# GLA/retention decoder layer on Trainium2: down projections of two MLP groups as seven products, with the weights' sums made in memory by GpSimd's transfers

## The chip, the cores and the metric

The kernel runs on one core of one Trainium2 chip, in one launch. The metric is the device time of the launch in microseconds (us), on that core. A difference is judged by the median of several runs.

## The reference

One inference step of a decoder layer, D = 1024, for 512 prompt tokens and 8 x 8 sample tokens (576 tokens in all), in fp32:

```python
def layer(x, pos, s_gla, s_ret, mem_k, mem_v, ...):
    m, s_gla_new, s_ret_new = mixer_block(rmsnorm(x, g_pre_mix), ...)   # GLA and retention branches, 4 heads each
    x = x + rmsnorm(m, g_post_mix)
    x = x + rmsnorm(cross_attn(rmsnorm(x, g_pre_xa), mem_k, mem_v, w_xq, w_xo), g_post_xa)
    hf = rmsnorm(x, g_pre_ffn)
    x = x + rmsnorm(jnp.square(jax.nn.relu(hf @ w_up)) @ w_down, g_post_ffn)
    return x, s_gla_new, s_ret_new
```

The change concerns the last line but one: `w_up` is 1024 x 4096, `w_down` 4096 x 1024. Beside the tokens' output the layer returns the new states and the keys and values of the memory.

## The kernel before, in words

Activations lie transposed: features over the 128 partitions, 8 blocks (k) of them, and 576 tokens in two halves of 288 (NH). Every fp32 product is three fp32r matmuls: a factor is split into hi (a cast on ScalarE, L94) and lo (the rest, a subtraction on VectorE, L95), and hi x hi, lo x hi, hi x lo add up in PSUM (`mm3`, L251 to L253).

Weights come in tiles of 128 x 1024 (512 KB). `plan` lists them in the order of use; `wfetch` (L180) has SP load the next into a ring of 6 tiles (`wraw`), `wsplit` makes its hi and lo (`wh`, `wl`, a ring of 3), `wnext` hands out the next split tile, and `gemm_m` does 48 matmuls with it, on both halves of the tokens.

The stages in order: keys and values of the memory; eight mixer units (one head of GLA or of retention each, `UNITS`, in `mixers`); the mixer's output, cross attention; and the MLP in four groups of 1024 hidden features. In a mixer unit GpSimd does small work between the other engines' steps: the causal mask on the scores (an affine select, L978), the reciprocal roots `rs` (a power, L887), `ks` (L1076), the lo part of q (L99), a product on the gate G (L1140) and the sum into `merged` (L1149). A unit forms keys `kf`, values `vt`, then the first pair of gate products (L1133) and the second.

MLP group 0 is done plainly. For groups 1 to 3 the up products (h = relu(x w)^2) use seven products in place of eight (`sevenfold`, L281), Winograd's form of Strassen's scheme: the weights' features and the tokens' features are taken as 2 x 2 blocks, the tokens in two halves. With sums S1 to S4 of the activation's blocks (`fsh`, `fsl`, made once by `sums_f`) and sums of the weight's blocks, seven products of 12 matmuls each give the four result blocks, 84 matmuls for each of the four b of a group. The weight sums are made on VectorE there: `begin` takes two raw tiles and does four subtractions of 128 x 512 (`minus`, L213); two of the splits go to an extra tile `wq`. The down projections of groups 1 and 2 are plain, 8 k of 48 matmuls, each added into the accumulator `y3` by VectorE (L655); group 3's down products and the last norm end the kernel.

What sets the order is the program and a scheduler behind it, which takes each engine's instructions in program order in the main, but lets independent ones pass each other.

Of the kernel before, what the change touches and what calls it, by code (L numbers as in the profile page):

```python
# [13 lines left out]
P = 128  # L14
KT = 8
# [11 lines left out]


RING, STAY, RAW, SEVEN = 0, 1, 2, 3
# [29 lines left out]
def decoder_step(ctx, tc, xT, memT, ktc, vc, s_gla, s_ret, w_in, w_ga, w_a2, w_mix, w_xq, w_xk, w_xv, w_xo,  # L59
                 w_up, w_ups, w_down, vecs, cst, gam, y_out, mk_out, mv_out, sg_p, sr_p, sg_s, sr_s):  # L60
# [110 lines left out]
    wq = []  # L171
    units = []

    def wfetch():
        if plan and sum(m == SEVEN for _, m in raws) < 2:
            src, mode = plan.pop(0), RING
            if isinstance(src, tuple):
                src, mode = src
            raw = wp.tile([P, 1024], F32, name="wraw", bufs=N_RAW)
            nc.sync.dma_start(out=raw if len(src.shape) == 2 else raw.rearrange("p (k n) -> p k n", n=src.shape[2]), in_=src)  # L180
            raws.append((raw, mode))

    def wsplit():
        if units:
            units.pop(0)()
        elif raws:
            if raws[0][1] == SEVEN:
                begin()
                return
# [4 lines left out]
            pool = staying[-1] if mode == STAY else wp  # L194
            wh = pool.tile([P, 1024], F32R, name="wh")
            wl = pool.tile([P, 1024], F32R, name="wl")
            split(wh, wl, raw)
            ready.append((wh, wl))

    def halves(w):  # L200
        return w.rearrange("p (q n) -> p q n", q=2)

    def begin():


        while len(raws) < 2:
            wfetch()
        p0, p1 = (raws.pop(0)[0] for _ in range(2))
        t = wp.tile([P, 1024], F32, name="wraw", bufs=N_RAW)
        q0, q1, qt = halves(p0), halves(p1), halves(t)  # L210

        def minus(out, a, b):
            nc.vector.tensor_tensor(out=out, in0=a, in1=b, op=ALU.subtract)  # L213

        def ring(raw):
            wh = wp.tile([P, 1024], F32R, name="wh")
            wl = wp.tile([P, 1024], F32R, name="wl")
            split(wh, wl, raw)
            ready.append((wh, wl))

        def own(raw, o, n):
            w = wq[0][:, o:o + n], wq[0][:, o + n:o + 2 * n]
            split(*w, raw)
            ready.append(w)

        def unit_a():
            ring(p0)
            wfetch()

        units.extend([unit_a, lambda: ring(t), lambda: own(p1, 0, 1024),  # L230
                      lambda: minus(q1[:, 0], q1[:, 0], qt[:, 0]), lambda: own(q1[:, 0], 2048, 512)])
# [3 lines left out]
        wfetch()  # L235

    def wnext(n=P):

        while sum(len(r) == 2 for r in ready) < 2 and (raws or plan):
            while not units and plan and len(raws) + sum(len(r) == 1 for r in ready) < N_RAW - 1:  # L240
                n0 = len(raws)
                wfetch()
                if len(raws) == n0:
                    break
            if not raws and not units:
                break
# [26 lines left out]
    def sevenfold(x, p1, p5, u2, c11, c22, c12, c21):  # L273
# [375 lines left out]
    xnp = ctx.enter_context(tc.tile_pool(name="xnp", bufs=2))  # L649
# [4 lines left out]
    def add(out, a, b, op=ALU.add):  # L654
        nc.vector.tensor_tensor(out=out, in0=a, in1=b, op=op)  # L655

    def sums_f():

        for j in range(4):
# [5 lines left out]
            add(c2[:, 1], c2[:, 0], c2[:, 1])  # L665
            add(c2[:, 0], c1[:, 0], c2[:, 0], ALU.subtract)
            add(c1[:, 0], c2[:, 1], c1[:, 0], ALU.subtract)
            add(c1[:, 1], c1[:, 1], c1[:, 0], ALU.subtract)
            yield
            split(fsh[:, 2:4, j], fsl[:, 2:4, j], c2)  # L670
            split(fsh[:, 0:2, j], fsl[:, 0:2, j], c1)
            yield

    FQ = {"A11": (fh, fl, 0), "A12": (fh, fl, 1), "A22": (fh, fl, 3),
# [760 lines left out]
```

## Time and profile before

| what | us |
|---|---|
| median of 3 runs | 1197.8 (1197.7 to 1197.8) |
| the profiled execution | 1200.96 |
| its span, first to last instruction | 1199.2 |
| TensorE (PE) busy | 1168.2 |
| VectorE (DVE) busy | 747.2 |
| ScalarE (ACT) busy | 564.1 |
| GpSimd (POOL) busy | 152.7 |

The span is what the trace shows; the profiled execution's time holds it and what lies around it. Busy time is the sum over an engine's instructions with overlaps counted once; PE stands for matmuls, PEld for the loads of the stationary operand, SP for the engine that issues DMAs. L253 is line 253 of the kernel before; a tile's name stands in rows without its number.

### The profile page before, as it was taken

The numbers are of one execution on the slowest core, as the hardware profiler recorded it, in microseconds if no ns is written. First come the engines' busy times: TensorE is split into PE (matmuls) and PEld (weight loads), VectorE is DVE, ScalarE is ACT, GpSimd is POOL, SyncE is SP. The second block draws the span as 40 slices with busy tenths as digits, with TensorE's granted clock in tenths as the row PEclk, the third lists the DMA queues.
The fourth block names the chain that finished last, engine by engine and source line by source line (L and its number), as shares of the span: only waits on it lengthen the run. The fifth ranks groups of instructions, "written<-read, shape, count | busy, mean of one in ns | idle before, by whom it ended". The sixth has DMA issues, their size and how long they took to land.

```text
span 1199.2 us, 22007 instructions
## 1 busy us (share of the span) xinstructions
PE 1168.2 (97%) x9022; PEld 1134.6 (95%) x9022; DVE 747.2 (62%) x1334; ACT 564.1 (47%) x993; POOL 152.7 (13%) x165
## 2 busy tenths in 40 slices
PE   8999999999999999999999989999999999999995
PEld 7899999999999999999999878889999999999995
DVE  6756657566746574757777545686937546456565
ACT  5534546443444344524564534556527416515652
POOL 0521213122312231221001000000000000000000
PEclk9999999999999999999999999999999999999998
DMA  8762424232424232422745677653223223321631
GB/s 291 244 213 89 128 80 137 75 125 88 128 71 143 74 128 89 128 89 76 231 130 159 226 233 238 222 164 123 88 71 105 89 71 103 109 71 56 217 108 60
DMA packets 65621, 157.98 MB, mean 132 GB/s; under 512 B 5648, under 2 KB 34576, under 8 KB 65392
## 3 DMA queue, kind: packets, MB, share of 16 engines
q1 hardware_dynamic: 65520, 156.57, 41.0%
q8 instruction: 71, 1.16, 0.4%
q14 instruction: 30, 0.25, 0.1%
HBM read 140.29 MB, written 16.25 MB: 131 GB/s over the span
## 4 chain that ended last, share of the span: by engine, by line
PE 89%; DVE 4%; DMA 2%; ACT 2%; issue 1%; POOL 1%; SPq 0%; POOLq 0%; DVEq 0%; ACTq 0%
PE psg L251 22%; PE psg L252 22%; PE psg L253 22%; PE psa L281 6%; PE psg L281 3%; PE psa L251 2%; PE pso L281 2%; PE psa L252 1%; PE psa L253 1%; DMA wraw<-in_w_xo 1%; PE pso L1254 1%; DVE wl L95 1%; PE psa L1097 1%; PE pso L1092 1%; DVE res L527 1%
## 5 line engine op out<-in xcount | busy, mean ns | idle before, releaser
L251 PE MATMUL psg<-xh,wh 128*128 128x288 f32 x1280 | 381.5, 298 | 0.4 <-DVE t L819 0.3
L252 PE MATMUL psg<-xh,wl 128*128 128x288 f32 x1280 | 377.9, 295 | 0.8 <-DVE wl L95 0.8
L253 PE MATMUL psg<-xl,wh 128*128 128x288 f32 x1280 | 377.8, 295 | 0.0
L95 DVE TENSOR_TENSOR wl<-wraw,wh 128x1024 fp32r<-128x1024 f32 x196 | 241.8, 1234 | 93.0 <-ACT wh L94 92.3
L94 ACT CAST wh<-wraw 128x1024 fp32r<-128x1024 f32 x196 | 206.0, 1051 | 187.5 <-PE psg L253 105.7
L251 PEld LDWEIGHTS psg<-xh,wh 128*128 128x128 f32 x1280 | 240.8, 188 | 3.5 <-issue 2.2
L252 PEld LDWEIGHTS psg<-xh,wl 128*128 128x128 f32 x1280 | 240.9, 188 | 1.1 <-DVE wl L95 1.0
L253 PEld LDWEIGHTS psg<-xl,wh 128*128 128x128 f32 x1280 | 240.6, 188 | 0.1
L251 PE MATMUL psg<-hh,wh 128*128 128x288 f32 x512 | 152.2, 298 | 0.7 <-DVE y L761 0.6
L252 PE MATMUL psg<-hh,wl 128*128 128x288 f32 x512 | 150.6, 295 | 0.3 <-DVE wl L95 0.3
L253 PE MATMUL psg<-hl,wh 128*128 128x288 f32 x512 | 150.7, 295 | 0.0
L251 PEld LDWEIGHTS psg<-hh,wh 128*128 128x128 f32 x512 | 96.1, 188 | 1.6 <-issue 1.1
L252 PEld LDWEIGHTS psg<-hh,wl 128*128 128x128 f32 x512 | 96.0, 188 | 0.6 <-DVE wl L95 0.6
L253 PEld LDWEIGHTS psg<-hl,wh 128*128 128x128 f32 x512 | 96.1, 188 | 0.0
L333 POOL TENSOR_TENSOR rs<-ms,mhalf 96x3 f32<-96x3 f32 (+1 forms) x11 | 11.0, 999 | 525.1 <-DVE ms L326 525.1
L955 ACT COPY vt<-psg 128x512 f32<-128x512 f32 x16 | 9.4, 587 | 77.5 <-PE psg L253 77.5
L887 POOL TENSOR_TENSOR rs<-mv,mhalf 128x1 f32<-128x1 f32 x48 | 29.8, 621 | 112.7 <-DVE mv L882 64.6
L957 DVE COPY vd<-psg 128x128 f32<-128x128 f32 x32 | 7.8, 286 | 55.6 <-ACT vt L955 55.6
L251 PE MATMUL psg<-bh,wh 128*128 128x288 f32 x128 | 38.4, 300 | 1.6 <-ACT wh L94 1.1
L252 PE MATMUL psg<-fh,wl 128*128 128x288 f32 x128 | 38.9, 304 | 1.0 <-DVE wl L95 1.0
L655 DVE TENSOR_TENSOR y<-psg,y 128x576 f32<-128x576 f32 x16 | 12.1, 757 | 44.4 <-PE psg L253 44.4
L251 PE MATMUL psg<-fh,wh 128*128 128x288 f32 x128 | 39.0, 305 | 0.2 <-ACT fh L94 0.2
(331 smaller groups left out, 2413.0 us busy)
## 6 DMA issues: line engine op xcount, KB each, us to landing
wraw<-in_w_in SPq DMA_DIRECT2D x64, 512.0 KB, 3.7
wraw<-in_w_down SPq DMA_DIRECT2D x38, 512.0 KB, 4.3
wraw<-in_w_ups SPq DMA_DIRECT2D x24, 512.0 KB, 3.7
wraw<-in_ktc SPq DMA_DIRECT2D x16, 512.0 KB, 5.0
wraw<-in_vc SPq DMA_DIRECT2D x16, 512.0 KB, 4.5
wraw<-in_w_xq SPq DMA_DIRECT2D x14, 512.0 KB, 4.3
wraw<-in_w_xo SPq DMA_DIRECT2D x14, 512.0 KB, 6.4
wraw<-in_w_up SPq DMA_DIRECT2D x14, 512.0 KB, 4.5
```

Source lines behind the costliest of these rows:

```text
L94: nc.scalar.copy(hi, src)
L95: nc.vector.tensor_tensor(out=lo, in0=src, in1=f32(hi), op=ALU.subtract)
L251: nc.tensor.matmul(out, ah, bh, start=first, stop=False)
L252: nc.tensor.matmul(out, al, bh, start=False, stop=False)
L253: nc.tensor.matmul(out, ah, bl, start=False, stop=last)
L281: nc.tensor.matmul(out, s[:, q, k], m[:, k], start=first and k == i == 0, stop=k == 3 and i == 2, skip_group_check=True)
L527: nc.vector.tensor_tensor(out=res[:, kk, c], in0=y[:, kk], in1=rj, op=ALU.add)
L655: nc.vector.tensor_tensor(out=out, in0=a, in1=b, op=op)
L887: nc.gpsimd.tensor_tensor(out=rs[:t], in0=mv[:t], in1=mhalf[:t, 0:1], op=ALU.pow)
L1092: nc.tensor.matmul(so[32 * j:32 * j + 8, o], qsd[:, b * 8:b * 8 + 8], s0[:, j], start=False, stop=True, skip_group_check=True, tile_positi ...
L1097: nc.tensor.matmul(U[:, j * 256:(j + 1) * 256], kst[g][:, 2 * bp + j, :], vst[g], start=True, stop=True)
L1254: nc.tensor.matmul(acc[rows, :256], x(h), w[:, h], start=first, stop=last, skip_group_check=True, tile_position=(0, 32 * h))
```

## The change

The sums of the weights are no longer made by VectorE at their use. The host lays out the weights of five groups of products (up 1, down 1, up 2, down 2, up 3) as blocks b11, b12, b21, b22 of 20 b (`w_sev`). During the mixers GpSimd issues DMAs from memory to memory that form, for ten pairs of b, three sums per b in internal tensors `t_sev`: t1 = b11 + b12, t2 = (t1 + b22, b12 + b22), t4 = t2[0] + b21. A pair takes eight transfers of 512 KB (64 x 2048 elements): four copies and four that add to what lies there. `sums` is called four times in each mixer unit and issues the steps that `SUMS_AT` and `SUM_STEPS` give for that call. A pair begins with a copy of one fresh element of the tile just made (`pace`) and its transfer of 1 x 1 into each of two sums' places, which the next copies overwrite.

With the sums in memory, `sevenfold` reads its weights as tiles of two 128 x 512 blocks (60 half-tile loads from `w_sev`, 80 from `t_sev`; a fourth tile of each b holds t4 alone, mode LAST), and it is now also used for the down projections of groups 1 and 2. Their activation is h: A11 and A12 go to `ha`, A22 to a free part of `fh`, the sums S1 to S4 to `hh` and `hl` (`pairs`). The seven products come in another order, and in a down group's first b A12 comes straight after A11 (`late`). `begin`, `units` and `wq` are gone. In all there are 8607 matmul instructions instead of 8703; GpSimd's queue goes from 170 instructions to 280, SP's from 347 to 447.

```diff
-RING, STAY, RAW, SEVEN = 0, 1, 2, 3
+RING, STAY, RAW, LAST = 0, 1, 2, 3
+N_SEV = 20
+SUMS_AT = (2, 5, 7, 10, 12, 15, 17, 20, 22, 25)
+SUM_STEPS = (0, 0, 1, 1, 2, 3, 4, 5)
...
-    def seven(w, b0):
-        return [(w[b0 + b][:, kh], SEVEN) for b in range(4) for kh in range(2)]
+    def seven(b0):
+        out = []
+        for n in range(b0, b0 + 4):
+            g, i = n // 2, n % 2
+            b = [w_sev[q, n] for q in range(4)]
+            t1, t2, t4 = t_sev[g]
+            out += [((b[0], t1[i]), RING), ((t2[0, i], t2[1, i]), RING), ((b[2], b[3]), RING), ((t4[i],), LAST)]
+        return out
     plan += whole(w_up) + rest(whole(w_up), 0) + whole(w_down)
     for g in range(1, 4):
-        plan += seven(w_ups, 4 * (g - 1))
-        plan += whole(w_down, 4 * g) + (rest(whole(w_down, 12), 0) if g == 3 else [])
+        plan += seven(8 * (g - 1))
+        plan += seven(8 * g - 4) if g < 3 else whole(w_down, 4) + rest(whole(w_down, 4), 0)
+    steps = {}
+    for g, at in enumerate(SUMS_AT):
+        b11, b12, b21, b22 = (w_sev[q, 2 * g:2 * g + 2] for q in range(4))
+        t1, t2, t4 = t_sev[g]
+        for n, (dst, src, plus) in zip(SUM_STEPS, (
+                (t1, b11, 0), (t2[1], b12, 0), (t1, b12, 1), (t2[1], b22, 1),
+                (t2[0], t1, 0), (t2[0], b22, 1), (t4, t2[0], 0), (t4, b21, 1))):
+            steps.setdefault(at + n, []).append((dst, src, plus))
+    clock = [0]
+    pace = perm.tile([1, 1], F32, name="pace")
+    def sums(after):
+        if clock[0] in SUMS_AT:
+            t1, t2, _ = t_sev[SUMS_AT.index(clock[0])]
+            nc.gpsimd.tensor_copy(pace, after[0:1])
+            for t in (t1[0], t2[1, 0]):
+                nc.gpsimd.dma_start(out=t[0:1, 0:1], in_=pace)
+        for dst, src, plus in steps.pop(clock[0], ()):
+            nc.gpsimd.dma_start(out=dst, in_=src, max_dma_last_dim=8192, **({"accum_op": ALU.add} if plus else {}))
+        clock[0] += 1
...
+            if isinstance(src, tuple):
+                for i, t in enumerate(src):
+                    nc.sync.dma_start(out=raw[:, i * 512:(i + 1) * 512], in_=t)
...
+            n = 512 if mode == LAST else 1024
+            pool = wdp[0] if mode == LAST else staying[-1] if mode == STAY else wp
+            wh = pool.tile([P, n], F32R, name="wh")
+            wl = pool.tile([P, n], F32R, name="wl")
+            split(wh, wl, raw[:, :n])
...
-        minus(qt[:, 1], q1[:, 1], q0[:, 1])
-        minus(q0[:, 1], q0[:, 1], q0[:, 0])
-        minus(qt[:, 0], q1[:, 1], q0[:, 1])
...
+        def c11():
+            prod(b, wb, 0, "A12", True)
+            add(c1[:, 0], b, c1[:, 0])
         prod(acc, wa, 0, "A11", True)
-        p1(acc)
-        while units:
-            wsplit()
+        nc.scalar.copy(c1[:, 0], acc)
+        if late:
+            c11()
+        prod(c, wa, 1, "S1", True)
+        nc.scalar.copy(c2[:, 1], c)
+        wmore()
         wd = ready.pop(0)
-        prod(c, wa, 1, "S1", True)
-        p5(c)
-        if raws and raws[0][1] == SEVEN:
-            begin()
         prod(acc, wc, 0, "S2", False)
-        wsplit()
-        u2(acc)
-        prod(b, wb, 0, "A12", True)
-        more()
-        c11(b)
+        nc.scalar.copy(c1[:, 1], acc)
+        wmore()
+        prod(c, wb, 1, "S4", False)
+        add(c1[:, 1], c, c1[:, 1], ALU.subtract)
         prod(acc, wc, 1, "S3", False)
-        c22(acc)
-        prod(c, wb, 1, "S4", False)
-        c12(c)
-        more()
+        add(c2[:, 1], c2[:, 1], acc, ALU.subtract)
+        done22()
+        wmore()
+        if not late:
+            c11()
+        done1()
+        wmore()
         prod(acc, wd, 0, "A22", False)
-        more()
-        c21(acc)
+        done21(acc)
...
+    def pairs(c1, c2, sh, sl):
+        add(c2[:, 1], c2[:, 0], c2[:, 1], ALU.subtract)
+        add(c2[:, 0], c1[:, 0], c2[:, 0], ALU.subtract)
+        split(sh[:, 2:4], sl[:, 2:4], c2)
+        add(c1[:, 0], c2[:, 1], c1[:, 0], ALU.subtract)
+        add(c1[:, 1], c1[:, 1], c1[:, 0])
+        split(sh[:, 0:2], sl[:, 0:2], c1)
...
+        plain = g in (0, 3)
+        ha = None if plain else biga.tile([P, 2, 2, 4, NH], F32R, name="ha", tag="biga")
+        def xh7(n):
+            if n in SQ:
+                return hh[:, SQ[n]], hl[:, SQ[n]]
+            return (fh[:, 2], fl[:, 2]) if n == "A22" else (ha[:, 0, n == "A12"], ha[:, 1, n == "A12"])
...
+            def done22():
+                relu2(c2[:, 1])
+                if not plain:
+                    split(fh[:, 2, b], fl[:, 2, b], c2[:, 1])
+            def done1():
+                relu2(c1)
+                split(*((hh[:, 0:2, b], hl[:, 0:2, b]) if plain else (ha[:, 0, :, b], ha[:, 1, :, b])), c1)
+            def done21(ps):
+                relu2(c2[:, 0], ps)
+                if plain:
+                    split(hh[:, 2:4, b], hl[:, 2:4, b], c2)
+                else:
+                    pairs(c1, c2, hh[:, :, b], hl[:, :, b])
+            sevenfold(xf7, c1, c2, done1, done22, done21)
+        if plain:
+            break
+        for b in range(4):
+            c1, c2 = (hp.tile([P, 2, NH], F32, name="hr") for _ in range(2))
+            y = [y3[:, 2 * b:2 * b + 2, hc(half)] for half in range(2)]
+            def done21(ps):
+                nc.scalar.copy(c2[:, 0], ps)
+                add(y[1], y[1], c2)
+            sevenfold(xh7, c1, c2, lambda: add(y[0], y[0], c1), lambda: None, done21, b == 0)
...
+            sums(kf[:, 511:512])
...
+            sums(vt[:, 1, 511:512])
...
+            sums(G[:, 1, NT - 1:])
```

The places in the engines' queues where the transfers and the new products came to stand. First GpSimd, in the mixer unit from about 208 us of the trace on, before (ql is the lo part of q, sm the scores, klo and ks parts of the key):

```order
L99 TENSOR_TENSOR ql_2563<-qf_2561,qh_2562 128x512 [waits Activation_49]
L978 AFFINE_SELECT sm_2785<-sm_2785 128x128 [waits Activation_49]
L1076 TENSOR_TENSOR ks_2816<-klo_2811,cm_834 128x512 [waits DVE_49]
L978 AFFINE_SELECT sm_2850<-sm_2850 128x128 [waits Activation_49,Pool_49]
L1076 TENSOR_TENSOR ks_2880<-klo_2875,cm_834 128x512 [waits DVE_49,PE_49]
```

The same stretch with the change:

```order
L102 TENSOR_TENSOR ql_2588<-qf_2586,qh_2587 128x512 [waits Activation_49]
L201 DMA t_sev20<-in_w_sev 64x2048 [waits DMASW6_49]
L201 DMA t_sev21<-in_w_sev 64x2048 [waits DMASW7_49]
L201 DMA t_sev21<-t_sev20 64x2048 [waits DMASW0_49]
L201 DMA t_sev21<-in_w_sev 64x2048 [waits DMASW3_49,DMASW2_49]
L201 DMA t_sev22<-t_sev21 64x2048 [waits DMASW3_49]
L1003 AFFINE_SELECT sm_2815<-sm_2815 128x128 [waits Activation_49]
L1101 TENSOR_TENSOR ks_2846<-klo_2841,cm_835 128x512 [waits DVE_49]
L201 DMA t_sev22<-in_w_sev 64x2048 [waits DMASW4_49]
L1003 AFFINE_SELECT sm_2880<-sm_2880 128x128 [waits Activation_49]
L1101 TENSOR_TENSOR ks_2910<-klo_2905,cm_835 128x512 [waits DVE_49,PE_49]
```

Five transfers have come between ql and the first mask, and a sixth between the first `ks` and the second mask; each of them waits in the queue for earlier ones (DMASW). The next rows of GpSimd's queue, from the unit's masks on to its first roots, before:

```order
L978 AFFINE_SELECT sm_2942<-sm_2942 128x128 [waits Activation_49,Pool_49]
L887 TENSOR_TENSOR rs1_2933<-mv_2930,mhalf_85 128x1 [waits DVE_49]
L978 AFFINE_SELECT sm_3034<-sm_3034 128x128 [waits Activation_49]
L887 TENSOR_TENSOR rs1_3025<-mv_3022,mhalf_85 128x1 [waits DVE_49]
L887 TENSOR_TENSOR rs1_3116<-mv_3113,mhalf_85 128x1 [waits DVE_49,Pool_49]
L887 TENSOR_TENSOR rs1_3141<-mv_3138,mhalf_85 128x1 [waits DVE_49,Pool_49]
```

With the change:

```order
L1003 AFFINE_SELECT sm_2972<-sm_2972 128x128 [waits Activation_49,Pool_49]
L910 TENSOR_TENSOR rs1_2963<-mv_2960,mhalf_85 128x1 [waits DVE_49]
L197 COPY pace_112<-G_2778 1x1 [waits DVE_49]
L199 DMA t_sev30<-pace_112 1x1 [waits Pool_49]
L1003 AFFINE_SELECT sm_3064<-sm_3064 128x128 [waits Activation_49]
L199 DMA t_sev31<-pace_112 1x1
L910 TENSOR_TENSOR rs1_3055<-mv_3052,mhalf_85 128x1 [waits DVE_49]
L201 DMA t_sev30<-in_w_sev 64x2048 [waits DMASW6_49]
L201 DMA t_sev31<-in_w_sev 64x2048 [waits DMASW7_49,DMASW1_49]
L910 TENSOR_TENSOR rs1_3153<-mv_3150,mhalf_85 128x1 [waits DVE_49]
L910 TENSOR_TENSOR rs1_3178<-mv_3175,mhalf_85 128x1 [waits DVE_49,Pool_49]
```

The next pair's first element, its two transfers and the pair's first two copies now stand between the masks and the roots (`rs`).

The third place is TensorE at the border from group 1's up products to its down projection, before (`psg` is the accumulator of a plain product):

```order
L251 MATMUL psg_11291<-hh_10785,wh_11214 128x288
L252 MATMUL psg_11291<-hh_10785,wl_11215 128x288
L253 MATMUL psg_11291<-hl_10786,wh_11214 128x288
L251 MATMUL psg_11291<-hh_10785,wh_11214 128x288 [waits Activation_49]
L252 MATMUL psg_11291<-hh_10785,wl_11215 128x288
L251 MATMUL psg_11347<-hh_10785,wh_11287 128x288 [waits DVE_49]
L252 MATMUL psg_11347<-hh_10785,wl_11288 128x288
L253 MATMUL psg_11347<-hl_10786,wh_11287 128x288
```

With the change, from the last A22 matmul on (`psa_11480` takes A11, `pso_11481` A12; `ha` and `hh` hold h):

```order
L280 MATMUL psa_11340<-fl_9469,wh_11371 128x288
L280 MATMUL psa_11480<-ha_10903,wh_11391 128x288
L280 MATMUL psa_11480<-ha_10903,wl_11392 128x288
L280 MATMUL psa_11480<-ha_10903,wh_11391 128x288 x2
L280 MATMUL psa_11480<-ha_10903,wl_11392 128x288
L280 MATMUL psa_11480<-ha_10903,wh_11391 128x288 x2
L280 MATMUL psa_11480<-ha_10903,wl_11392 128x288
L280 MATMUL psa_11480<-ha_10903,wh_11391 128x288
L280 MATMUL pso_11481<-ha_10903,wh_11452 128x288 [waits DVE_49,Activation_49]
L280 MATMUL pso_11481<-ha_10903,wl_11453 128x288 [waits DVE_49]
L280 MATMUL pso_11481<-ha_10903,wh_11452 128x288 x2
L280 MATMUL pso_11481<-ha_10903,wl_11453 128x288
```

and six rows on:

```order
L280 MATMUL pso_11481<-ha_10903,wh_11452 128x288 x2
L280 MATMUL pso_11481<-ha_10903,wl_11453 128x288
L280 MATMUL pso_11481<-ha_10903,wh_11452 128x288
L280 MATMUL psa_11480<-ha_10903,wh_11391 128x288 [waits Activation_49]
L280 MATMUL psa_11480<-ha_10903,wl_11392 128x288
L280 MATMUL pso_11481<-ha_10903,wh_11452 128x288
```

Before, the matmul that waits for the fourth block (k of block b = 3) is passed by the next k's; now A11's first three blocks and A12's come first, and A11's fourth behind them.

## Rows read from the trace of the kernel before

**Rows 1.** The page: its span and the engines' busy time.

```profile
span 1199.2 us, 22007 instructions
...
PE 1168.2 (97%) x9022; PEld 1134.6 (95%) x9022; DVE 747.2 (62%) x1334; ACT 564.1 (47%) x993; POOL 152.7 (13%) x165
```

Columns of the next group: stretch, its length, busy us of PE, PEld, DVE, ACT, POOL (instructions), granted clock, DMA share, GB/s.

**Rows 2.** Busy time by stretch, the MLP: a down stage, the up stage behind it.

```profile
938.00:990.00 52.00, 52.00 (x393) 51.86 (x392) 24.30 (x30) 12.33 (x16) 0.00 (x0) 1.00 0.20 62
990.00:1035.00 45.00, 45.00 (x337) 44.75 (x337) 30.23 (x40) 29.55 (x51) 0.00 (x0) 1.00 0.39 118
```

A row of a timeline has the start, the duration, engine, line, operation, out<-in, sizes and count; in brackets the idle time before it and what ended that.

**Rows 3.** TensorE's timeline at the borders of the stages.

```profile
893.03 0.29 PE L281 MATMUL psa<-fh,wh 128*128 128x288 f32 x1
...
938.28 0.29 PE L281 MATMUL psa<-fl,wq 128*128 128x288 f32 x1
938.41 0.30 PE L251 MATMUL psg<-hh,wh 128*128 128x288 f32 x1
...
989.57 0.29 PE L281 MATMUL psa<-fh,wh 128*128 128x288 f32 x1
...
1034.64 0.30 PE L251 MATMUL psg<-hh,wh 128*128 128x288 f32 x1
...
1085.80 0.29 PE L281 MATMUL psa<-fh,wh 128*128 128x288 f32 x1
```

**Rows 4.** The timeline of ScalarE and VectorE behind the up stage of group 1.

```profile
940.15 1.24 ACT L94 CAST hh<-hr 128x576 fp32r<-128x576 f32 x2
...
940.84 1.43 DVE L95 TENSOR_TENSOR hl<-hr,hh 128x576 fp32r<-128x576 f32 x2 [2.76 <-ACT hh L94]
```

A row of the waits: what waited, for what; us in all, times, the longest.

**Rows 5.** TensorE's waits, 70 to 560 us, then 893 to 1086 us.

```profile
PE psa L969 <- ACT T L1008: 0.8, 1, 0.8
PE psg L251 <- DVE t L819: 0.3, 1, 0.3
...
PE psa L281 <- ACT hr L727: 0.2, 1, 0.2
```

**Rows 6.** VectorE's subtractions on raw weights: ns of one (least, median, most).

```profile
L213 DVE TENSOR_TENSOR wraw<-wraw x48: 680/692/695, 859.5 to 1120.5; 128x512 f32<-128x512 f32 x48
```

**Rows 7.** SP's queue: its longest wait.

```profile
SPq L180 <- DVE wl L95: 658.0, 139, 12.3
```

**Rows 8.** GpSimd's timeline in the mixer unit from 208 us on.

```profile
208.07 1.29 POOL L99 TENSOR_TENSOR ql<-qf,qh 128x512 fp32r<-128x512 f32 x1 [5.28 <-ACT qh L98]
226.17 0.29 POOL L978 TENSOR_SCALAR_AFFINE_SELECT sm<-sm 128x128 f32<-128x128 f32 x1 [16.82 <-ACT sm L977]
...
254.48 0.55 POOL L887 TENSOR_TENSOR rs<-mv,mhalf 128x1 f32<-128x1 f32 x1 [2.42 <-DVE mv L884]
255.75 0.55 POOL L887 TENSOR_TENSOR rs<-mv,mhalf 128x1 f32<-128x1 f32 x1 [0.72 <-DVE mv L885]
```

**Rows 9.** TensorE and VectorE in the same unit: who uses mask and root.

```profile
233.89 0.28 PE L251 MATMUL psa<-vh,sh 128*128 128x256 f32 x1
...
257.80 0.38 PE L1029 MATMUL psa<-idn,on 128*128 128x128 f32 x2
...
256.34 0.48 DVE L893 TENSOR_SCALAR on<-pso,rs 128x256 f32<-128x256 f32 x1 [0.73 <-POOL rs L887]
```

**Rows 10.** The timeline where the first and last fresh element are made.

```profile
115.46 0.82 DVE L1133 SCALAR_TENSOR_TENSOR G<-psg,vec,t 128x576 f32<-128x576 f32 x1 [2.07 <-ACT t L1132]
...
470.82 0.59 ACT L955 COPY vt<-psg 128x512 f32<-128x512 f32 x1 [4.83 <-PE psg L253]
```

**Rows 11.** DMA issues: count, KB each, median us from issue to landing.

```profile
wraw<-in_w_in SPq DMA_DIRECT2D x64, 512.0 KB, 3.7
...
wraw<-in_w_xk SPq DMA_DIRECT2D x8, 512.0 KB, 7.4
...
res<-out_y SPq DMA_DIRECT2D x8, 288.0 KB, 5.5
...
vec<-in_vecs SPq DMA_DIRECT2D x1, 38.0 KB, 1.8
```

**Rows 12.** Busy time by stretch, in the mixers.

```profile
200.00:250.00 50.00, 50.00 (x394) 48.86 (x393) 30.16 (x72) 25.70 (x53) 9.16 (x13) 1.00 0.32 100
```

**Rows 13.** VectorE's copies, 100 to 520 us: busy us, mean ns, idle time before.

```profile
L922 DVE COPY qf<-t 128x512 f32<-128x512 f32 x3 | 1.3, 427 | 4.0 <-POOL t L903 4.0
```

More of the change, by code (lines that the diff above doesn't have):

```diff
@@ L170, in decoder_step @@
     raws, ready, staying = [], [], []
-    wq = []
-    units = []
+    wdp = []
     def wfetch():
-        if plan and sum(m == SEVEN for _, m in raws) < 2:
+        if plan:
             src, mode = plan.pop(0), RING
-            if isinstance(src, tuple):
+            if isinstance(src, tuple) and isinstance(src[1], int):
                 src, mode = src
             raw = wp.tile([P, 1024], F32, name="wraw", bufs=N_RAW)
-            nc.sync.dma_start(out=raw if len(src.shape) == 2 else raw.rearrange("p (k n) -> p k n", n=src.shape[2]), in_=src)
+            if isinstance(src, tuple):
+                for i, t in enumerate(src):
+                    nc.sync.dma_start(out=raw[:, i * 512:(i + 1) * 512], in_=t)
+            else:
+                nc.sync.dma_start(out=raw if len(src.shape) == 2 else raw.rearrange("p (k n) -> p k n", n=src.shape[2]), in_=src)
@@ L181, in wfetch @@
             raws.append((raw, mode))
     def wsplit():
[L184 to L187, printed above, removed]
-                begin()
-                return
+        if raws:
             raw, mode = raws.pop(0)
@@ L193, in wsplit, with wmore @@
                 return
[L194 to L197, printed above, removed]
+            n = 512 if mode == LAST else 1024
[3 more added lines that the diff above has]
+            split(wh, wl, raw[:, :n])
             ready.append((wh, wl))
[L200 to L206, printed above, removed]
+    def wmore():
+        while plan and len(raws) < N_RAW - 1:
             wfetch()
[L208 to L231, printed above, removed]
-        minus(qt[:, 1], q1[:, 1], q0[:, 1])
-        minus(q0[:, 1], q0[:, 1], q0[:, 0])
-        minus(qt[:, 0], q1[:, 1], q0[:, 1])
-        wfetch()
+        wsplit()
     def wnext(n=P):
         while sum(len(r) == 2 for r in ready) < 2 and (raws or plan):
-            while not units and plan and len(raws) + sum(len(r) == 1 for r in ready) < N_RAW - 1:
-                n0 = len(raws)
+            while plan and len(raws) + sum(len(r) == 1 for r in ready) < N_RAW - 1:
                 wfetch()
-                if len(raws) == n0:
-                    break
-            if not raws and not units:
+            if not raws:
                 break
@@ L664, in sums_f @@
             yield
[L665 to L668, printed above, removed]
+            pairs(c1, c2, fsh[:, :, j], fsl[:, :, j])
             yield
[L670 to L674, printed above, removed]
-          "S2": (fsh, fsl, 0), "S4": (fsh, fsl, 1), "S3": (fsh, fsl, 2), "S1": (fsh, fsl, 3)}
+    SQ = {"S2": 0, "S4": 1, "S3": 2, "S1": 3}
     def xf7(n):
-        h, l, q = FQ[n]
-        return h[:, q], l[:, q]
+        return (fsh[:, SQ[n]], fsl[:, SQ[n]]) if n in SQ else tuple(
+            t[:, {"A11": 0, "A12": 1, "A22": 3}[n]] for t in (fh, fl))
     y3 = None
@@ L1141, in unit @@
                 tick()
+            sums(G[:, 1, NT - 1:])
             def finish():
@@ L1411 @@
         "w_xv": np.ascontiguousarray(x["w_xv"][0].reshape(2, 4, P, 4, 256).transpose(3, 2, 0, 1, 4)), "w_xo": blocks(x["w_xo"][0]),
-        "w_up": blocks(wu[:, :1024]), "w_ups": sevens(wu[:, 1024:]),
-        "w_down": np.concatenate([blocks(wd[g * 1024:(g + 1) * 1024]) for g in range(4)]),
+        "w_up": blocks(wu[:, :1024]),
+        "w_sev": np.concatenate([sevens(wu[:, 1024:2048]), sevens(wd[1024:2048]), sevens(wu[:, 2048:3072]),
+                                 sevens(wd[2048:3072]), sevens(wu[:, 3072:])], axis=1),
+        "w_down": np.concatenate([blocks(wd[:1024]), blocks(wd[3072:])]),
         "vecs": np.ascontiguousarray(vecs), "cst": const,
```

62 lines of the change are left out of this document (23 added, 39 removed).

## Prediction, made before the result was seen

> **What bounds the kernel now.** I read the totals first: TensorE is busy for 97% of a span of 1199.2 us [rows 1], so what counts is how many matmuls there are and whether any of them waits. Then the stretches of the MLP: in the down projection of group 1 TensorE is busy for all of 52 us and in the up products of group 2 for all of 45, at a granted clock of 1.00, which is the upper of the two levels, 2.4 GHz [rows 2]. The TensorE timeline gives the borders of these stages [rows 3]: up products of group 1 from 893.03 to 938.41 (45.38 us), its down projection to 989.57 (51.16), up products of group 2 to 1034.64 (45.07), its down projection to 1085.80 (51.16). The down projection issues 8 x 48 = 384 matmuls, 0.133 us each; the up products issue 4 x 84 = 336, 0.134 to 0.135 each. Nothing else sets the pace there. From 70 to 560, nearly all of it the mixers, TensorE waits for others for about 1 us [rows 5], so that stretch is bound by matmuls too, but with GpSimd in its chains.
>
> **Part 1: two down projections as seven products.** 96 matmuls go from 768. By count that is 96 x 0.133 = 12.8 us. I take the stage that already works in this way: 51.16 - 45.07 = 6.09 for each group, 12.2 for two. Ends: 11.6 (by group 1's 45.38) and 12.8. All of it is on the path, as TensorE is the path. **-12.2.**
>
> **Part 2: the crossing from up to down.** The sums of h are formed only when the last product of block b = 3 is out. Before, its last matmul starts at 938.28 and ends 0.29 later [rows 3], and ScalarE's two casts to hi start at 940.15, 0.62 each, VectorE's lo at 940.84, 0.72 each [rows 4]: hi is there 2.2 us behind the last matmul, lo 3.0. TensorE filled that time with other matmuls. Now the same chain has a cast more ahead of it (A22's own) and two subtractions behind. In TensorE's new order 9 matmuls of A11 and 9 of A12 stand behind the last A22 matmul ahead of the first that waits for block 3: 18 x 0.133 = 2.4 us of cover. I put the first hi at 2.7 us (2.2 and half a microsecond for the cast), the lo and the sums at 3.4 to 4.1, with more matmuls between. That leaves 0.3, and some 0.3 each for two later places: 1.0 per crossing. Ends: 0, and 4 us each where nothing covered it. **+2.0** for two.
>
> **Part 3: what VectorE, ScalarE and SP lose and gain.** 48 subtractions of 0.69 us leave VectorE [rows 6], 33 us of work. TensorE waited for none of them: from 893 to 1086 it waited 0.2 us in all, for ScalarE [rows 5]. So it is worth **0**; what hides it is the 45 us of matmuls in an up stage, beside 30 us of VectorE [rows 2]. SP issues 140 half tiles for 40 whole ones. Its weight loads wait for ring slots for 658 us in all [rows 7], that is, each is ready before its slot; the added issues run in that time: **0**. If that cover were gone the price is one landing of 3.7 us [rows 11] in a stage.
>
> **Part 4: GpSimd's transfers in the mixers.** 80 transfers of 512 KB, 20 of one element and 10 copies of one element are added in GpSimd's queue, and each waits there for the one it depends on; GpSimd's own instructions stand behind it. No transfer of GpSimd, none from memory to memory and no accumulating one is in the trace. The nearest rows: 3.7 us from issue to landing for a 512 KB load at ease, 7.4 for the same in the crowded start, 5.5 for a read of what was written to memory [rows 11]. No row bounds it from above; 7.4 is the farthest. I call the mean of a step s, from issue to landing, and take 5: nearest to the 5.5, the one row that has to do with data written to memory in the same run, and a little less since half of the steps only copy.
>
> How much room is there? A pair is six steps deep (first element, copy, accumulate, copy, accumulate, copy, accumulate). The first fresh element is G at 116.3, the last vt at 471.4 [rows 10]: 355 us for nine intervals, 39.5 each. With 1.8 us for a one-element transfer (the 38 KB load, [rows 11]) and 0.5 for copy and issue, 37.2/6 = 6.2 us is the step that still fits. At s = 5 every pair is done before the next begins.
>
> Where GpSimd's other work is concerned there are two kinds of places. In a GLA unit the mask (affine select) can stand behind five transfers that follow ql. Ql ends at 209.4, the mask starts at 226.17 as its scores come only then, and TensorE wants the product at 233.89 [rows 8, 9]. Three waits of 5 us end at 225: the mask is on time, and even three of 7 us are inside the 24 us. The reciprocal roots (rs), in units of both kinds, also come to stand behind transfers. There the room is small: rs of 255.75 ends at 256.3, VectorE's product runs 256.34 to 256.82, TensorE takes it at 257.80 [rows 8, 9], 1.0 us. Where a one-element transfer's 1.8 us falls just ahead, 0.8 is lost; ten pairs make 8 us at most. Mostly GpSimd idled 2.4 us and more ahead of rs, so I take a quarter: **+2.0**, ends 0 and 8 (a gain is excluded: nothing is taken from GpSimd there).
>
> The transfers also share the DMA engines. In the mixers these are busy for 0.32 of the time, moving 100 GB/s [rows 12]. 80 x 524 KB are 42 MB, over 390 us 107 GB/s more; if an accumulating transfer, half of them, counts twice, 161. By the same row that is 0.34 to 0.52 on top: an estimated share of 0.66 to 0.84. Loads would then land later than 3.7 us, perhaps at 7.4; SP waits up to 12.3 us for a slot with nothing else to do [rows 7], so I take 0 for that.
>
> **A rule that speaks against it.** VectorE's copies in the mixers are few and short: qf's take 427 ns each, three in 420 us [rows 13]. The Trainium skill, "SBUF — State Buffer", the box on the "DVE blocks DMA" trap, says that a transfer issued by GpSimd cannot have its descriptors written while VectorE runs a two-port operation such as an fp32 copy inside SBUF. No run here shows it; by such copies it would cost under 1 us and leave the sum alone, but if it held for VectorE's other passes, it would lengthen each step, which is the first rival below.
>
> **Sum.** -12.2 + 2.0 + 0 + 2.0 = -8.2. The profiled execution took 1200.96 us, 3.2 above the median of the runs shown (1197.8); it would come to 1192.8, and the median to **1189.6**. The forecast's own range: -12.8 with nothing lost, 1185.0, to -11.6 + 8 + 1 = -2.6, 1195.2 (one of the two losses at its end, the other at half of what I took).
>
> **Rivals.**
> (1) GpSimd's chain becomes the bound. With a step over 6.2 us every pair ends late, and the lateness adds up, since the next pair and all of GpSimd's masks and roots queue behind it: nine times 6 x (s - 6.2), less the 7 us of slack of a mask. At s = 7 that is 43 - 7 = 36, about 1226; at the 7.4 of [rows 11] it is 58, about 1247. It cancels the gain at 54 (s - 6.2) - 7 = 8.2, s = 6.5. For it: every step reads what the last one wrote, on engines that would be busy for 0.66 to 0.84, and no row shows such a step. Against it: three of the four transfers in [rows 11] land in under 6.2 us.
> (2) GpSimd is late in moderation: s between 6.3 and 6.5, or the roots late by 0.8 at most places. Then the loss is 6 to 14, and the time 1194 to 1202, about no change.
> (3) The crossings are not covered, or the sums of h wait for ScalarE's weight casts: 4 us each, 8 in all in place of 2: 1195.6.
> (4) The change does not do what it says: the down stages stay near 51 us, for instance since a product waits for its weights' sums. The sums end near 505 us, far ahead of the first use at 893, so this needs the loads to be late in the stage: three and a half tiles, 1.84 MB, for each b in 11.3 us are 163 GB/s, above the 62 of the down stage and the 118 of the up stage [rows 2]. About 1198.
>
> **How the numbers follow.** No change means within 0.2%, 2.4 us, about what a measurement of this kernel can tell (1195.4 to 1200.2). The forecast has 0.60. Rival 1 has 0.19, rival 2 has 0.13 (0.04 faster, 0.05 same, 0.04 slower), rival 3 has 0.04 (half faster, half same), rival 4 has 0.04 (same). So faster 0.66, same 0.11, slower 0.23. The range must leave out no more than 2 in 10: rival 1 lies above 1203 but for its lowest part, so 1185 to 1204; the forecast's own range is 1185.0 to 1195.2.
>
> **What would show it.** In the profile after: down stages of groups 1 and 2 of about 45 us, in 336 matmuls; behind the last A22 of an up stage a gap of about 1 us and none of 4; no subtractions on raw weights; the mixers' end no more than 2 us later. GpSimd's transfers should land in 4 to 6 us. Right for rival 1 would be TensorE waits for the mask or rs of tens of us and a mixers' end 30 us later, with GpSimd's idle time ended by its own transfers. My prediction is wrong if a step takes over 6.5 us, or if transfers of weights in the mixers get so late that TensorE waits for hi or lo parts.

## The result: slower by 0.55%, and the profile after

The change took 1206.1 us, median of 4 runs (1203.5 to 1209.7), against 1197.8 before (1197.7 to 1200.2 in these runs): a ratio of 1.0055, 95% interval 1.0038 to 1.0073. I had forecast 1189.6. Its times spread by 6 us. Three of the four of the kernel before agree to the tenth here, but in the later runs that kernel's times spread by 4.7 to 6.6 us as well.

The profiled execution is the fastest of the four (1203.5 us). Its page, with the DMA issues at the end:

```profile
span 1201.8 us, 22374 instructions
...
PE 1162.6 (97%) x8926; PEld 1125.3 (94%) x8926; DVE 769.3 (64%) x1374; ACT 595.5 (50%) x1069; POOL 216.8 (18%) x275
...
wraw<-in_w_in SPq DMA_DIRECT2D x64, 512.0 KB, 5.4
t_sev<-in_w_sev POOLq DMA_DIRECT2D x60, 512.0 KB, 6.3
wraw<-t_sev SPq DMA_DIRECT2D x80, 256.0 KB, 2.8
...
t_sev<-t_sev POOLq DMA_DIRECT2D x20, 512.0 KB, 4.8
...
t_sev<-pace POOLq DMA_DIRECT2D x20, 0.0 KB, 2.4
```

The borders of the stages on TensorE's timeline, as in [rows 3]: the first up product of group 1, the first down product (A11, from `ha`) of group 1 and of group 2, and the first plain matmul behind group 3's up products:

```profile
907.70 0.29 PE L280 MATMUL psa<-fh,wh 128*128 128x288 f32 x1
...
952.49 0.30 PE L280 MATMUL psa<-ha,wh 128*128 128x288 f32 x1
...
1042.76 0.30 PE L280 MATMUL psa<-ha,wh 128*128 128x288 f32 x1
...
1133.01 0.30 PE L250 MATMUL psg<-hh,wh 128*128 128x288 f32 x1
```

From the first up product of group 1 to the end of group 3's these stages now take 225.31 us. Before they began at 893.03 and ended here:

```profile
1130.88 0.30 PE L251 MATMUL psg<-hh,wh 128*128 128x288 f32 x1
```

237.85 us, so the MLP gained **12.5 us**. But it begins 14.7 us later, at 907.70 and not 893.03. Lined up product by product, 1.1 of that had come up by 96 us, before the first transfer; 13.4 came between 96 and 566 us of the trace before, in the mixers; 0.2 behind them. The mixers by their busy time, before and then after (columns as in [rows 2]):

```profile
120.00:520.00 400.00, 400.00 (x3128) 392.19 (x3126) 247.36 (x564) 179.54 (x359) 94.70 (x99) 1.00 0.34 107
```

```profile
120.00:520.00 400.00, 391.90 (x3034) 380.71 (x3033) 249.92 (x554) 176.19 (x353) 152.61 (x203) 1.00 0.76 207
```

TensorE, which had no gap there, now has 8.1 us of them; GpSimd is busy for 58 us more; the DMA share went from 0.34 to 0.76. What GpSimd waits for, and what TensorE waits for, from 70 to 570 us:

```profile
POOL t_sev L201 <- DMA t_sev<-in_w_sev: 82.3, 23, 7.6
...
POOL t_sev L201 <- DMA t_sev<-t_sev: 48.0, 16, 5.2
...
POOL t_sev L201 <- DMA t_sev<-pace: 12.6, 8, 3.2
```

```profile
PE psa L1142 <- DVE on L916: 2.8, 3, 1.2
PE psa L1122 <- DVE on L914: 2.1, 2, 1.4
PE psa L994 <- DVE vl L98: 1.4, 1, 1.4
PE psa L1054 <- DVE on L914: 1.0, 2, 0.7
...
PE psa L994 <- ACT wh L97: 0.7, 1, 0.7
```

GpSimd stands at transfers that wait for a landing for 143 us. Of TensorE's 13 waits in this stretch, 9.7 us in all, 7 with 5.9 us end with VectorE's `on`, the product with the root. One such place, GpSimd first, then VectorE, then TensorE:

```profile
388.37 0.56 POOL L910 TENSOR_TENSOR rs<-mv,mhalf 128x1 f32<-128x1 f32 x1 [1.43 <-DVE mv L907]
391.30 0.61 POOL L201 DMA_DIRECT2D t_sev<-t_sev  x1 [2.36 <-DMA t_sev<-in_w_sev]
391.91 0.57 POOL L910 TENSOR_TENSOR rs<-mv,mhalf 128x1 f32<-128x1 f32 x1
```

```profile
389.37 0.14 DVE L908 TENSOR_SCALAR mv<-mv 128x1 f32<-128x1 f32 x1
392.52 0.48 DVE L916 TENSOR_SCALAR on<-pso,rs 128x256 f32<-128x256 f32 x1 [3.01 <-POOL rs L910]
```

```profile
393.06 0.44 PE L1142 MATMUL psa<-idn,on 128*128 128x128 f32 x2 [1.18 <-DVE on L916]
```

The variance `mv` is there at 389.51, but the transfer ahead of the root waits until 391.30 for the accumulation before it; the root starts 2.4 us late, more than the 1.0 us of room that [rows 8, 9] showed, and TensorE stands for 1.18 us. The other waits for `on` are of 0.4 to 1.4 us.

Masks were late too. The 1.4 us for `vl` are a wait at 367.47 us; `vl` stands in VectorE's queue behind `sl`, a part of the masked score, and the mask stood behind a transfer that waited. It starts 19.7 us behind the end of ql, where it was 16.8 before:

```profile
359.09 0.53 POOL L201 DMA_DIRECT2D t_sev<-t_sev  x1 [5.99 <-DMA t_sev<-in_w_sev]
...
361.15 0.31 POOL L1003 TENSOR_SCALAR_AFFINE_SELECT sm<-sm 128x128 f32<-128x128 f32 x1
```

```profile
361.83 0.29 DVE L98 TENSOR_TENSOR sl<-sm,sh 128x128 fp32r<-128x128 f32 x1 [3.11 <-ACT sh L97]
```

The wait for `wh` at 238.20 us has the same form, through ScalarE's queue. The waits listed make 9.7 of the 13.4 us; the rest stands in no row of waits.

### The profile page after: what moved, and what is told of

It reads as the page before. It is cut to its first block, busy times and chain, and to the rows that moved or that the text cites. A ratio compares the mean times of both kernels' runs of the same rounds, so it can differ in the third digit from the quotient of the medians.

```text
span 1201.8 us, 22374 instructions
## 1 busy us (share of the span) xinstructions
PE 1162.6 (97%) x8926; PEld 1125.3 (94%) x8926; DVE 769.3 (64%) x1374; ACT 595.5 (50%) x1069; POOL 216.8 (18%) x275
## 4 chain that ended last, share of the span: by engine, by line
PE 72%; DMA 10%; DVE 7%; issue 5%; POOL 3%; ACT 2%; SPq 0%; POOLq 0%; DVEq 0%; ACTq 0%
PE psg L251 15%; PE psg L250 15%; PE psg L252 15%; PE psa L280 11%; PE psg L280 5%; DMA t_sev<-in_w_sev 4%; PE pso L280 3%; DMA t_sev<-t_sev 3%; DVE wl L98 2%; PE psa L250 1%; PE psa L251 1%; PE psa L252 1%; DMA wraw<-in_w_xo 1%; PE pso L1281 1%; POOL t_sev L201 1%
## 5 line engine op out<-in xcount | busy, mean ns | idle before, releaser
L98 DVE TENSOR_TENSOR wl<-wraw,wh 128x1024 fp32r<-128x1024 f32 (+1 forms) x236 | 286.1, 1213 | 113.8 <-ACT wh L97 109.0
L97 ACT CAST wh<-wraw 128x1024 fp32r<-128x1024 f32 (+1 forms) x236 | 239.2, 1014 | 150.4 <-PE psg L252 60.0
L250 PE MATMUL psg<-hh,wh 128*128 128x288 f32 x256 | 76.0, 297 | 0.7 <-DVE y L784 0.6
L251 PE MATMUL psg<-hh,wl 128*128 128x288 f32 x256 | 75.5, 295 | 0.3 <-DVE wl L98 0.3
L252 PE MATMUL psg<-hl,wh 128*128 128x288 f32 x256 | 75.4, 295 | 0.0
L201 POOL DMA_DIRECT2D t_sev<-in_w_sev x60 | 43.5, 749 | 85.0 <-DMA t_sev<-t_sev 48.0
L250 PEld LDWEIGHTS psg<-hh,wh 128*128 128x128 f32 x256 | 48.0, 188 | 1.2 <-issue 1.1
L251 PEld LDWEIGHTS psg<-hh,wl 128*128 128x128 f32 x256 | 48.1, 188 | 0.6 <-DVE wl L98 0.6
L252 PEld LDWEIGHTS psg<-hl,wh 128*128 128x128 f32 x256 | 48.0, 188 | 0.2 <-DVE hl L98 0.2
```

The costliest lines, as they stand in the source:

```text
L97: nc.scalar.copy(hi, src)
L98: nc.vector.tensor_tensor(out=lo, in0=src, in1=f32(hi), op=ALU.subtract)
L201: nc.gpsimd.dma_start(out=dst, in_=src, max_dma_last_dim=8192, **({"accum_op": ALU.add} if plus else {}))
L250: nc.tensor.matmul(out, ah, bh, start=first, stop=False)
L251: nc.tensor.matmul(out, al, bh, start=False, stop=False)
L252: nc.tensor.matmul(out, ah, bl, start=False, stop=last)
```

## Experiments

The time of the kernel before differs by a few us between the chips that were used (medians 1197.8 to 1200.9), so each run is compared by its ratio to that kernel on the same chip at the same time, with the 95% interval in brackets.

**Without the sums.** The products read stored blocks in the sums' places, so the result lacks the sums; no transfer is issued.

```diff
-            t1, t2, t4 = t_sev[g]
+            t1, t2, t4 = (b[1], b[1]), ((b[0], b[0]), (b[3], b[3])), (b[2], b[2])
...
     def sums(after):
+        return
```

> Leaves out the weights' sums: GpSimd issues no transfer, and the products read stored blocks where the sums would stand; loads, splits and matmuls stay as in the change. Every theory of the mixers' loss (waits in GpSimd's queue, the time of issuing, contention for the DMA engines) expects the whole gain of the MLP and no loss: 1197.8 - 12.5 = 1185.3, within 1184 to 1187. Above 1190 part of the loss would have nothing to do with the transfers.

1186.4 us, 0.9898 (0.9883 to 0.9912): the MLP's gain alone. All of the loss belongs to the transfers, directly or by what they do to the schedule.

**Small transfers.** Each transfer moves 8 of 128 partitions' rows; sums left out as above.

```diff
-            nc.gpsimd.dma_start(out=dst, in_=src, max_dma_last_dim=8192, ...)
+            nc.gpsimd.dma_start(out=dst[:, :8], in_=src[:, :8], max_dma_last_dim=8192, ...)
```

> Each of the 80 transfers moves 32 KB instead of 512 KB, the same chain of waits; the products read stored blocks, so the sums are left out. Waits theory: a step falls from 5.9 us to 2.5 to 3, and the loss of 13 to 20 us to 2 to 6: 1187 to 1191. Issuing theory: 110 instructions of 0.5 to 0.8 us in GpSimd's queue remain, the loss stays: 1198 to 1205. Contention theory: no traffic is left: 1185 to 1186.

1267.3 us, 1.0564 (1.0545 to 1.0584): slower than everything, against all three theories. Beside the sums left out only the size of the transfers was changed, and TensorE's products stand in quite another order. That the scheduler goes by an estimate of durations, transfers included, is my reading of this and not shown. The mixers lost some 80 us, at a granted clock of 0.94 in the mean from 120 to 520 us. As a test of the waits this run says nothing, but it put the order of the other engines on the list of suspects.

**Held at three places.** No one-element transfers; each transfer held (an edge that orders the queue, no wait) behind a GpSimd instruction: behind ql or the second rope sum, the second `ks`, the last gate product.

```diff
+        with tc.issue_after(last):
+            for dst, src, plus in steps.pop(clock[0], ()):
+                nc.gpsimd.dma_start(out=dst, in_=src, ...)
```

> All 80 transfers in full, but each held behind a chosen instruction of GpSimd's queue, three places in a unit (behind q's lo part or the second rope sum; behind the second ks; behind the last gate product), a step of a pair's chain at each, so that a step has some 12 to 30 us to land before the next is issued; the one-element copies and transfers are gone. Waits theory: nothing is waited for, 1185 to 1189. Issuing theory: 80 of 110 issues remain, 9 us and more of loss: 1194 to 1200. Contention theory: the traffic is the same: 1198 to 1206.

1198.8 us, 0.9994 (0.9983 to 1.0006). By its time alone this run would fit the issuing theory or the contention theory; the next one speaks against both. GpSimd waits for no landing here, yet 11.5 us are gone: at the end of six of the eight units TensorE has two gaps,

```profile
196.75 0.41 PE L1050 MATMUL psa<-idn,on 128*128 128x128 f32 x2 [0.87 <-DVE mv L905]
197.00 0.38 PE L1140 MATMUL psa<-idn,on 128*128 128x128 f32 x2
197.94 0.44 PE L1140 MATMUL psa<-idn,on 128*128 128x128 f32 x2 [0.56 <-DVE on L913]
```

and its rows stand in another order than without transfers: the gate products, which without transfers fill the time in which the last roots are made, have run out by then. No transfer stands ahead of these roots in GpSimd's queue. So I put this loss down to the order, which is an argument from these rows and no test; order and waits had to be taken apart.

**Six places, nothing else moved.** Ten transfers in a unit at six places, chosen so that every other instruction of TensorE, VectorE, ScalarE and GpSimd stands in the order of the kernel without sums.

```diff
+    CAPS = {'kf': (4, 12), 'ks0': (1, 15), 'rs0': (1, 9), 'rs1': (1, 7), 'vt': (1, 2), 'end': (3, 18)}
```

(how many transfers may go behind the named instruction, and the us that pass up to it by plan)

> All 80 transfers in full and the sums read, no one-element transfers; in each mixer unit ten transfers, held at six places of GpSimd's queue (four behind q's lo part or the second rope sum, one with the values, one behind the first ks, one each behind the first two roots, three behind the last gate product), dependent ones at least 8 us apart by plan; every other instruction of TensorE, VectorE, ScalarE and GpSimd stands in the same order as in the kernel without sums. Theory that the loss comes of waits and of the order that the scheduler makes of the other engines: nothing of either is left, 1186 to 1189. Issuing theory: 80 issues of 0.5 to 0.8 us remain, 1192 to 1199. Contention theory: the traffic is all there, 1197 to 1206.

1189.3 us, 0.9915 (0.9894 to 0.9937); run once more later, 1188.5, 0.9897 (0.9876 to 0.9918):

> The version with six chosen places once more, as the measure for the one-element transfers on the same chip, and to see its gain again: 0.7% to 1.1% faster than before.

This computes all that the change does, and is faster than both kernels. Its mixers:

```profile
120.00:520.00 400.00, 400.00 (x3128) 392.20 (x3127) 253.16 (x563) 179.62 (x359) 136.02 (x169) 1.00 0.71 197
```

TensorE is busy for all 400 us at a DMA share of 0.71, with 80 issues in GpSimd's queue. So neither the traffic nor the time of issuing makes the loss by itself. The places matter: this stretch of GpSimd's queue is the one of [rows 8].

```profile
211.30 3.77 POOL L204 DMA_DIRECT2D t_sev<-in_w_sev  x5
227.59 0.29 POOL L1008 TENSOR_SCALAR_AFFINE_SELECT sm<-sm 128x128 f32<-128x128 f32 x1 [12.52 <-ACT sm L1007]
...
239.19 0.56 POOL L913 TENSOR_TENSOR rs<-mv,mhalf 128x1 f32<-128x1 f32 x1 [1.80 <-DVE mv L911]
239.72 0.86 POOL L204 DMA_DIRECT2D t_sev<-in_w_sev  x1
242.78 0.29 POOL L1008 TENSOR_SCALAR_AFFINE_SELECT sm<-sm 128x128 f32<-128x128 f32 x1 [2.21 <-ACT sm L1007]
```

Five are issued in one go into the 16 us that GpSimd has free ahead of the first mask, one behind a root with some 5 us to the next; none waits.

**Waits at harmless places.** The same method, but dependent steps may follow at once, at nearly the same places (three behind ql or the rope sum and four behind the last gate product, and one behind the fourth root in place of the one with the values).

```diff
-                if any((g, d) not in done or now[0] - done[g, d] < 8 for d in PRE[n]) :
+                if any((g, d) not in done or now[0] - done[g, d] < 0 for d in PRE[n]) :
```

> As the run with six places, but a pair's steps follow each other as soon as the queue lets them, so that GpSimd stands waiting for a landing of 5 to 8 us at three or four of ten transfers in each unit, much as in the change; the order of the other engines is that of the kernel without sums but for a few rows. If the waits make the loss, 8 to 20 us come back: 1194 to 1206. If the order of the other engines makes it, it stays as in the run with six places, 1186 to 1190.

1189.8 us, 0.9920 (0.9903 to 0.9936), though GpSimd waits for landings for 91 us:

```profile
POOL t_sev L204 <- DMA t_sev<-in_w_sev: 64.7, 16, 7.7
...
POOL t_sev L204 <- DMA t_sev<-t_sev: 26.7, 8, 5.3
```

A wait in GpSimd's queue is not in itself a loss. Here two of them, of 7.7 and 4.4 us, follow ql, and the mask behind them still had to wait for its scores:

```profile
228.04 0.79 POOL L204 DMA_DIRECT2D t_sev<-in_w_sev  x1 [4.36 <-DMA t_sev<-t_sev]
229.45 0.29 POOL L1008 TENSOR_SCALAR_AFFINE_SELECT sm<-sm 128x128 f32<-128x128 f32 x1 [0.62 <-ACT sm L1007]
```

**The order alone, and the queue alone.** Two runs take the two suspects apart by extra edges that fix each engine's order from a table. The first has no transfers (the sums are left out) and TensorE, VectorE and ScalarE in the change's order; the second has the change's transfers at their places in GpSimd's queue, and every other instruction in the order of the kernel without sums.

```diff
+            for a, b in zip(order, order[1:]):
+                tc.add_manual_dep(b, a.name, mybir.DependencyInfo(mybir.DependencyClass.NoSync, ...), ...)
```

> No transfers and no sums, as in the run without sums, but TensorE's, VectorE's and ScalarE's instructions stand in exactly the order that they have in the change. If the order that the scheduler makes around the transfers costs by itself, the time is over the 1186 of the run without sums: from the change's trace, where TensorE's gaps at 174, 238, 367 and 498 us are not behind a late root, I expect 4 to 6 us: 1190 to 1192. If only the waits cost, 1186 to 1187.

> The change with all transfers, each at its place in GpSimd's queue behind the same instruction, the one-element ones too, but every other instruction of TensorE, VectorE, ScalarE and GpSimd in the order of the kernel without sums. If GpSimd's waits ahead of roots and key products cost by themselves, 8 to 14 us over the run without sums: 1194 to 1200. If the order is the cause, 1187 to 1190.

The change itself was run with them:

> The change itself once more, as the measure for the other three on the same chip: 0.2% to 0.9% slower than before by what was measured first.

| | no transfers | the change's queue on GpSimd |
|---|---|---|
| order of the kernel without sums | 0.9898 (0.9883 to 0.9912) | 1.0104 (1.0077 to 1.0131) |
| the change's order | 0.9928 (0.9908 to 0.9947) | 1.0067 (1.0042 to 1.0092) |

(The upper left one was run earlier, on another chip.) The order alone costs 0.3%, some 3.6 us; the queue alone 2.1%, some 25 us; both together 1.7%, 20 us. The mixers of the profiled executions, lined up product by product against the run without sums, say the same: from 96 to 566 us the order alone loses 3.6 us, the queue alone 24.4, both together 23.4 (this execution is the slowest of its six; the first one, the fastest of four, loses 13.1), waits at harmless places 2.3 and six places nothing. In the run with the order alone TensorE waits for no `on`, `vl` or `wh`: of the four places that the expectation names, those at 238 and 367 us, behind late masks, belong to the queue. So the queue is the larger part by far. The two do not add up; whether the same queue costs more without the scheduler's order stays open, as the two intervals overlap. My expectation for the queue was too low by half, as I had taken the two to add up. Its trace has the longest gap in the mixers of all runs, again a root behind a transfer that waits:

```profile
532.03 0.84 POOL L207 DMA_DIRECT2D t_sev<-in_w_sev  x1 [4.39 <-DMA t_sev<-t_sev]
532.65 0.81 POOL L933 TENSOR_TENSOR rs<-mv,mhalf 128x1 f32<-128x1 f32 x1
```

```profile
534.03 0.44 PE L1165 MATMUL psa<-idn,on 128*128 128x128 f32 x2 [4.81 <-DVE on L939]
```

**The change's plan, held.** One edit: each transfer of the change is held behind the last GpSimd instruction ahead of its call, so that the scheduler can't issue it some calls of `sums` early, as it did in the rows shown ahead of the prediction (five in a row ahead of a mask).

```diff
+            with tc.issue_after(last):
-            nc.gpsimd.dma_start(out=dst, in_=src, ...)
+                nc.gpsimd.dma_start(out=dst, in_=src, ...)
```

> The change with one edit: each 512 KB transfer is held behind the GpSimd instruction that stands last ahead of its call in the program, so that it can't be issued calls earlier than planned; the one-element transfers stay, and the scheduler orders the rest anew (some 150 of TensorE's rows differ from the kernel without sums, as many as in the change). If the early issue and its waits are the larger part of the loss, it falls by half or more: 1190 to 1196. If the order is, 1198 to 1206.

1194.6 us, 0.9956 (0.9940 to 0.9973): of the 1.7% that the transfers cost, 1.1 come back by that one edit. GpSimd's waits fell to 69 us, from 159 in the change on the same chip (143 in the first execution). The other engines' rows were ordered anew as well, so what of the gain and of the rest is due to waits and what to order this run does not tell.

**The one-element transfers.** Put back into the version with six places.

```diff
+                    nc.gpsimd.tensor_copy(pace, fresh[0:1])
+                    for t in (t_sev[g][0][0], t_sev[g][1][1, 0]):
+                        nc.gpsimd.dma_start(out=t[0:1, 0:1], in_=pace)
```

> The version with six chosen places, with the change's one-element copy and its two one-element transfers ahead of each pair's first copies put back (30 instructions in GpSimd's queue, each pair's first copy waits 1.5 to 6 us for them). If these waits cost wherever they stand: ten pairs by 1 to 2 us, 10 to 20 us over the version without. If a wait costs only ahead of a root or key product that is then late, which these places avoid: 0 to 2 us over it.

1188.0 us, 0.9890 (0.9868 to 0.9913), against 0.9897 without them on the same chip: they cost nothing there, though GpSimd waits 43 us for their landing:

```profile
POOL t_sev L214 <- DMA t_sev<-pace: 43.1, 10, 11.2
```

## Why the prediction was wrong, step by step

- **Part 1 and part 2 held, with one size off.** The MLP was to gain 12.2 less 2.0 for the crossings, 10.2; it gained 12.5. TensorE has no gap at either crossing: from 952.49 to 1042.76 a down and an up stage take 90.3 us, 672 matmuls at 0.134. The order does cover the whole wait for block 3, and the 1.0 us for each was too much.
- **Part 3 held.** No loss from splits or from SP's 140 half tiles (2.8 us to landing).
- **Part 4 failed, in its term for the roots.** "Where a one-element transfer's 1.8 us falls just ahead, 0.8 is lost; ten pairs make 8 us at most ... I take a quarter: +2.0". I priced only the one-element transfer ahead of a root, and once for a pair. But a pair has five more steps that wait, and the scheduler puts these ahead of roots, key products and masks as well. In place of 2.0 the mixers lost 13.4 us in the profiled execution, the fastest of the four, and 20 by the medians of the later runs; some 3 to 4 of that is the order. For the mask I took the 24 us until TensorE's product with the score as the room. The one at 361.15 us lies within them, 19.7 us behind ql, but VectorE's queue stood 3.1 us for it and was late with `vl`; the second mask of a unit I did not price. The rows to count were ahead of me: every row of GpSimd's queue in which a waiting transfer stands before a root, with the step's full wait and not the one-element transfer's, and against 1.0 us of room. The run that has only this queue shows it (25 us); the run with waits elsewhere (0.2% over no transfers) shows that it is the place that costs. That a long wait lowers the granted clock behind it, as shown at the end, was not in the sum at all.
- **The step was mis-sized by a little.** I took 5 us; transfers out of stored weights landed in 6.3, those between sums in 4.8, the median of all 80 being 5.9. By the budget of 39.5 us for each pair that still fits, and it did: pairs begin at 117.4 to 484.0 us, 40.7 apart. Rival 1, a chain that is the bound and late by more with each pair, did not come about. It was rival 2, roots that come late, to which I had given 6 to 14 us and a chance of 0.13. That its price could reach rival 1's lower end was missed, so the range ended at 1204.
- **What I left out:** that the scheduler would change the order of TensorE's rows in the mixers, and at a price: 0.3% here, and in the run with three places 11.5 us, if these are the order's.
- **Contention** was rightly put at zero: the loads of [rows 11] went from 3.7 to 5.4 us, and TensorE did not wait for them.
- **The rule of the Trainium skill** ("SBUF — State Buffer", the "DVE blocks DMA" box) stays open: no run took VectorE's copies away. The version with six places loses nothing with these copies in it.

## What to carry to other kernels

A transfer that waits in an engine's queue costs what the instruction behind it is late beyond its own room, so look for the engine's long idle stretches (here 13 to 17 us behind ql or the rope sum) and hold transfers there; in front of an instruction that is awaited within 1 us even one wait of 5 us is too much. A scheduler may move a transfer to such a place by itself: hold it with an ordering edge, and check that the order of the other engines did not move. Before judging what added work costs, run the version without it, and one with the same work in places where nothing is behind it.

## What the hardware showed that I had not expected

- Issuing takes GpSimd itself 0.56 to 0.75 us for each transfer in the mean, and no less for small ones: 43.5 us for 60 of 512 KB, 11.2 for 20 of them, 11.3 for the 20 of one element, in a list of lines from 70 to 575 us. These 66 us are as much as all of its 64 us of added busy time (in which overlaps count once), and with the six places they cost nothing.

```profile
L201 POOL DMA_DIRECT2D t_sev<-in_w_sev x60 | 43.5, 749 | 85.0 <-DMA t_sev<-t_sev 48.0 <-DMA t_sev<-in_w_sev 19.2 <-DMA t_sev<-pace 12.6
...
L199 POOL DMA_DIRECT2D t_sev<-pace x20 | 11.3, 573 | 3.4 <-POOL pace L197 3.4
```

- A transfer of 4 bytes takes 2.4 us to land in the change, one of 512 KB from memory to memory 4.8 (4.6 and 5.4 in the run with six places and the one-element transfers). The Trainium skill, "DMA: Bandwidth & Descriptors", Anatomy of one DMA — SWDGE (gpsimd) path, gives 2.0 us and the bytes over 436 GB/s for a transfer that GpSimd issues, an estimated 3.2 us for 512 KB. In the change the fixed part agrees nearly; the rest is 2.4 us and not 1.2 at a DMA share of 0.76, and 3.9 for the group in which 40 of the 60 transfers accumulate (6.3 us).
- A long wait of TensorE costs more than itself. In the change's later run the waits that end at 310.98, 372.44 and 529.39 us are 2.5, 2.7 and 4.0 us long, and the granted clock behind each is 0.50, that is 1.2 GHz, the lower of the two levels. In the first execution, whose longest wait in the mixers is 1.4 us, it stays at 1.00 there. First 3 us behind the 4.0 us wait, then 3 us behind the 1.18 us wait of the first execution (columns as in [rows 2]; 11 matmuls in the one, 23 in the other):

```profile
529.00:532.00 3.00, 2.61 (x11) 2.61 (x12) 3.00 (x4) 0.33 (x2) 1.19 (x1) 0.50 0.89 169
```

```profile
393.00:396.00 3.00, 2.94 (x23) 2.94 (x24) 3.00 (x4) 0.33 (x2) 1.01 (x2) 1.00 0.63 243
```
